# A two-layer encoder trunk in split-fp32 products: transposes of a pair's statistics reordered, last squares added by VectorE, operands and reloads hooked to other multiplies

## The chip, the cores and the metric

The kernel runs on one core of a Trainium2 chip. The metric is the device time of one execution in microseconds (us). A core has TensorE for matrix products (PE in the profile; PEld is its weight load), VectorE (DVE), ScalarE (ACT), GpSimd (POOL) and SyncE (SP), which here issues nearly all DMAs, in one order. Each engine runs its own instructions in order, and semaphores tie the engines together.

## What is computed

Two layers over 2048 tokens of width 1024, in float32, and a last norm:

```python
def reference(x, norm_even, w_in_even, conv_w, w_out_even, norm_odd, w_in_odd,
              q_gain, k_gain, w_out_odd, final_norm):
    for layer in range(DEPTH):                      # DEPTH = 2
        i = layer // 2
        if layer % 2 == 0:                          # short convolution and Fourier mixer
            x = x + short_conv_fourier_mixer(rms_norm(x, norm_even[i]), w_in_even[i], conv_w[i], w_out_even[i])
        else:                                       # grouped-query attention, 8 q heads, 2 kv heads
            x = x + gqa_axial_mixer(rms_norm(x, norm_odd[i]), w_in_odd[i], q_gain[i], k_gain[i], w_out_odd[i])
    return rms_norm(x, final_norm)

def rms_norm(x, g):
    return x * lax.rsqrt(jnp.mean(x * x, axis=-1, keepdims=True) + EPS) * g
```

Each mixer is one input projection, the mixing itself, and one output projection, whose result is added to x. The change concerns the first layer's output projection (with the residual add), the second layer's input projection, and the second layer's output projection. The norm that follows an output projection needs, for every token, the sum of the squares of its 1024 new values.

## The kernel before

**Products.** Tokens lie in four blocks of 512 (tb 0 to 3), and two blocks make a pair (pr 0 or 1). Activations are kept transposed (features on partitions). An operand is a float32 tile split in a high and a low part: ScalarE casts the high part (`split`, L42), VectorE subtracts it for the low part (L44). A product is three matmuls (L58, L59, L60). A projection is worked off in chunks: one pair of token blocks against 512 columns. A plain chunk has 8 block multiplies of 24 matmuls 128x512 each (a11 w11, a12 w21, a21 w11, a22 w21, a11 w12, ...). A fast chunk (`product`) does the same with 7 multiplies in the manner of Strassen and Winograd: the operands are "11", "s2", "s3", "s1", "12", "22", "s4", in this order, where s1 to s4 are sums and differences of the four blocks. Its results are finished in the order: block "22" (after the multiply s1), "11" (after 12), "21" (after 22), "12" (after s4). The first digit of a result block is the token block of the pair, the second the half of the columns.

**Where operands come from.** `load_block` loads a block of the activations (a11 and so on, two halves each) and splits it; `reload` hooks four such loads onto four multiplies of a chunk (a hook runs behind its multiply in program order). `prepare` returns four steps for a pair: s3a, s3b (the halves of s3 and s2, L285 on GpSimd, L288 on VectorE), s1 (L296 on GpSimd: block 22 + block 21, two halves) and s4 (L304 on GpSimd: block 12 minus s2, which is stored in DRAM in between as s2_y0 and so on). In each of them one source block is loaded straight into the operand's own tile and the other into a place of a ring with three places (ring_o). There are nine large tiles: two are the rings (ring_o, and ring_r for raw weights), seven are operands. So in a plain chunk whose four blocks are all live, three of the four combined operands have a tile at once, and the fourth one's loads wait for the last multiply that reads a block that is given up (a21).

**Statistics.** `out_chunk` adds the residual to each result block, and for its two halves ScalarE squares them (L1035, into a tile sq of a pool with two buffers) and GpSimd adds the squares into a sum per token block, acc (L1037). When a pair's two chunks (mc 0 and 1) are done, `rstd(tb)` transposes the sum of a token block on TensorE (four transposes, pm_n, L96), VectorE reduces it, and GpSimd takes the power. In the first layer's output projection there are four chunks: 0 (pr 0, plain), 1 (pr 0, fast), 2 (pr 1, plain), 3 (pr 1, fast); rstd(0) and rstd(1) are hooked onto the first two multiplies of chunk 2. rstd(2) and rstd(3) are hooked onto the second and fourth multiply of the next stage's first chunk (a z chunk). The second layer's output projection has chunks 0 (plain), 1 (fast) and 2 (plain, rstd(0) behind its first and rstd(1) behind its third multiply), and then single columns.

**Order.** TensorE's order is the program's. The orders of the other engines and of the DMAs of SP come from a scheduler, so a hook that stands elsewhere can move other instructions too.

**Names.** po are results of an output projection (po_p, po_u, po_v, po_w are tiles of a fast chunk's running sums, L461; L1016 and L1018 add the residual), wo and w the weights' split tiles, a_y, as_y, a_x, as_x, a_o plain and combined operands of the three projections, pq and pz results of the q and z (gate) columns, ptq the transposes of q, yT, x1T, oT tensors in DRAM.

## Time and profile before

| | |
|---|---|
| median of 3 runs | 2344.59 us (2343.51 to 2349.03) |
| profiled execution | 2344.58 us, its span 2342.8 us |
| PE busy | 2251.1 us, 96% of the span |
| DVE busy | 1694.0 us, 72% |
| ACT busy | 1264.6 us, 54% |
| POOL busy | 720.9 us, 31% |
| mean granted clock of TensorE | 0.982 |

An instruction's row gives its start, its length, its engine and line, what it writes and reads, and in brackets how long its engine was idle just before it and what ended that. The profiled execution and the median differ by 0.01 us. What TensorE's busy time leaves of the span is 91.7 us.

### The profile page before, as it was taken

The numbers are of one execution on the slowest core, as the hardware profiler recorded it, in microseconds if no ns is written. First come the engines' busy times: TensorE is split into PE (matmuls) and PEld (weight loads), VectorE is DVE, ScalarE is ACT, GpSimd is POOL, SyncE is SP. The second block draws the span as 40 slices with busy tenths as digits, with TensorE's granted clock in tenths as the row PEclk, the third lists the DMA queues.
The fourth block names the chain that finished last, engine by engine and source line by source line (L and its number), as shares of the span: only waits on it lengthen the run. The fifth ranks groups of instructions, "written<-read, shape, count | busy, mean of one in ns | idle before, by whom it ended". The sixth has DMA issues, their size and how long they took to land. (4 is left out here: it accounts for less than half of the span.)

```text
span 2342.8 us, 34481 instructions
## 1 busy us (share of the span) xinstructions
PE 2251.1 (96%) x12330; PEld 1905.7 (81%) x12330; DVE 1694.0 (72%) x2557; ACT 1264.6 (54%) x2713; POOL 720.9 (31%) x458
## 2 busy tenths in 40 slices
PE   9999899998989899999999999999999999999988
PEld 7877678877768699899977888888888888888867
DVE  7967667679776546765657888788787787887755
ACT  5442332223343346555537777777777777776422
POOL 3566434343654315424501111000001100013532
PEclk9999999998999999999999999999999999999989
DMA  4245732175897744575476555555555555558873
GB/s 164 84 151 178 240 125 72 63 268 191 293 291 235 221 138 149 195 246 172 152 238 239 202 203 201 192 202 196 198 200 191 200 204 192 204 186 296 283 247 109
DMA packets 268028, 457.53 MB, mean 195 GB/s; under 512 B 26192, under 2 KB 146128, under 8 KB 266064
## 3 DMA queue, kind: packets, MB, share of 16 engines
q1 hardware_dynamic: 260976, 447.63, 56.0%
q0 software_dynamic: 1008, 6.55, 0.7%
q8 instruction: 98, 1.61, 0.3%
q10 hardware_dynamic: 5872, 1.14, 0.2%
q14 instruction: 74, 0.61, 0.1%
HBM read 228.67 MB, written 92.36 MB: 137 GB/s over the span
## 5 line engine op out<-in xcount | busy, mean ns | idle before, releaser
L1410 DVE TENSOR_REDUCE mx<-s 128x1 f32<-128x512 f32 x512 | 350.9, 686 | 173.1 <-PE s L60 172.8
L1429 ACT ACTIVATE praw<-s,nb,qs 128x512 f32<-128x512 f32 x512 | 400.7, 798 | 18.6 <-DVE nb L1419 12.5
L1452 ACT CAST pr<-t 128x512 fp32r<-128x512 f32 x512 | 290.2, 599 | 182.5 <-PE t L1440 182.5
L1456 DVE TENSOR_TENSOR pr<-t,pr 128x512 fp32r<-128x512 f32 x512 | 329.2, 679 | 7.5 <-ACT pr L1452 7.2
L1440 PEld LDWEIGHTS t<-ident_r,P 128*128 128x128 f32 x2048 | 202.0, 140 | 36.8 <-DVE pr L1456 1.1
L58 PE MATMUL s<-kv,aq 128*128 128x512 f32 x512 | 211.0, 412 | 2.8 <-DMA aq<-qT 1.5
L58 PE MATMUL o<-pr,kv 128*128 128x512 f32 x512 | 212.2, 415 | 0.1
L1440 PE MATMUL t<-ident_r,P 128*128 128x128 f32 x2048 | 203.7, 243 | 0.9 <-DVE pr L1456 0.9
L60 PE MATMUL o<-pr,kv 128*128 128x512 f32 x512 | 202.5, 396 | 0.0
L59 PE MATMUL o<-pr,kv 128*128 128x512 f32 x512 | 202.2, 395 | 0.0
L60 PE MATMUL s<-kv,aq 128*128 128x512 f32 x512 | 202.0, 394 | 0.0
L59 PE MATMUL s<-kv,aq 128*128 128x512 f32 x512 | 201.0, 392 | 0.0
L1501 POOL TENSOR_TENSOR az<-az,lb 128x512 f32<-128x512 f32 x32 | 59.1, 1846 | 438.5 <-DMA lb<-ld 438.5
L1508 POOL TENSOR_TENSOR az<-az,oc 128x512 f32<-128x512 f32 x32 | 41.3, 1291 | 288.6 <-ACT oc L1507 288.6
L1037 POOL TENSOR_TENSOR acc<-acc,sq 128x512 f32<-128x512 f32 x48 | 81.5, 1700 | 129.4 <-ACT sq L1035 113.8
L60 PEld LDWEIGHTS o<-pr,kv 128*128 128x128 f32 x512 | 96.3, 188 | 23.2
L60 PEld LDWEIGHTS s<-kv,aq 128*128 128x128 f32 x512 | 96.1, 188 | 22.4
L58 PEld LDWEIGHTS s<-kv,aq 128*128 128x128 f32 x512 | 95.9, 187 | 21.7 <-ACT praw L1429 3.2
L1429 ACT ACTIVATION_READ_ACCUMULATOR praw<-s,nb,qs 128x1 f32 x512 | 112.4, 220 | 0.0
L59 PEld LDWEIGHTS o<-pr,kv 128*128 128x128 f32 x512 | 96.6, 189 | 17.1
L59 PEld LDWEIGHTS s<-kv,aq 128*128 128x128 f32 x512 | 96.4, 188 | 17.1
L58 PEld LDWEIGHTS o<-pr,kv 128*128 128x128 f32 x512 | 96.1, 188 | 16.9 <-ACT oc L1507 0.2
(774 smaller groups left out, 6162.8 us busy)
## 6 DMA issues: line engine op xcount, KB each, us to landing
P<-praw SPq DMA_DIRECT2D x256, 512.0 KB, 3.2
ring_r<-w SPq DMA_DIRECT2D x80, 512.0 KB, 4.0
ring_o<-x_T SPq DMA_DIRECT2D x32, 512.0 KB, 4.8
ring_r<-wo SPq DMA_DIRECT2D x32, 512.0 KB, 7.6
qT<-ring_o SPq DMA_DIRECT2D x64, 256.0 KB, 2.9
aq<-qT SPq DMA_DIRECT2D x31, 512.0 KB, 4.6
a_x<-x1T SPq DMA_DIRECT2D x18, 512.0 KB, 6.1
as_y<-yT SPq DMA_DIRECT2D x16, 512.0 KB, 7.8
```

Of the source, the lines that this page charges most:

```text
L58: nc.tensor.matmul(ps, lh, rh, start=first, stop=False, skip_group_check=shared)
L59: nc.tensor.matmul(ps, lh, rl, start=False, stop=False, skip_group_check=shared)
L60: nc.tensor.matmul(ps, ll, rh, start=False, stop=last, skip_group_check=shared)
L1037: nc.gpsimd.tensor_tensor(a, a, sq, op=ALU.add)
L1410: self.nc.vector.tensor_reduce(st.mx[h][:, b:b + 1], st.banks[h, b][:], op=ALU.max, axis=AX.X)
L1429: self.exp = nc.scalar.activation(raw[:, b % 2], st.banks.pop((h, b))[:], AF.Exp, bias=st.nb[h][:], scale=self.c.qs[:, st.g[0], st.g[1], h ...
L1440: self.nc.tensor.transpose(pt[:, h * P:(h + 1) * P].bitcast(F32R), st.Ps[h // 2][:, h % 2, kt // 8, (kt % 8) * P:(kt % 8 + 1) * P], self.c ...
L1452: self.nc.scalar.copy(pr[:, 0], pt[:])
L1456: self.nc.vector.tensor_tensor(pr[:, 1], pt[:], pr[:, 0], op=ALU.subtract)
L1501: nc.gpsimd.tensor_tensor(zt, zt, rb[:].rearrange("p (t h) -> p h t", h=4), op=ALU.mult)
L1508: nc.gpsimd.tensor_tensor(st.zt[:], st.zt[:], o[:], op=ALU.mult)
```

## The change

Four things are changed.

- In a fast chunk the squares of the blocks "21" and "12" are added by VectorE, the others still by GpSimd (12 of 48 adds move).
- The transposes of a pair's sums change places: rstd(1) behind the first and rstd(0) behind the second multiply in chunk 2 of the first output projection, and the same in chunk 2 of the second one (the finishing of these blocks, `finish`, is exchanged with them). In the z chunk rstd(3) is behind the fourth and rstd(2) behind the sixth multiply.
- The steps of `prepare` are hooked elsewhere. First output projection: s3a, s3b, s4, s1 behind multiplies 2, 4, 6, 7 of the plain chunk (counted from 0; s3a, s3b, s1, s4 behind 0, 2, 4, 6 before). Second input projection: s3a, s3b, s1 behind 0, 2, 4 of the first q chunk (1, 3, 6 before), and s4 behind the multiply "11" of the fast z chunk (behind 6 of the second q chunk before).
- `reload` hooks its four blocks onto "s3", "12", "22", "s4" of a fast chunk (onto "11", "s2", "s3", "s1" before), and the load of block 2 for the last stage (x2_2, 2 MB) hooks onto "s1" (onto "22" before).

```diff
         def s4():
-            self.A.pop("21")
+            self.A.pop("21", None)
...
         if last:
-            A = dict(self.A)
+            A = {a: self.A[a] for a in A_OPS if a in self.A}
             self.A.clear()
         for a in ("11", "s2", "s3", "s1", "12", "22", "s4"):
             base = ps.get({"12": "11", "s4": "s1"}.get(a))
-            ps[a] = self.multiply(A.pop(a) if last else A[a], W[W_OPS[a]], f"{name}{a}", base, a in ("11", "s1"))
+            ps[a] = self.multiply((A if a in A else self.A).pop(a) if last else A[a], W[W_OPS[a]], f"{name}{a}", base, a in ("11", "s1"))
...
             if not first:
-                nc.gpsimd.tensor_tensor(a, a, sq, op=ALU.add)
+                eng = nc.vector if kind == "fast" and block in ("21", "12") else nc.gpsimd
+                eng.tensor_tensor(a, a, sq, op=ALU.add)
...
-            hooks = {0: s3a, 2: s3b, 4: s1, 6: s4}
+            hooks = {2: s3a, 4: s3b, 6: s4, 7: s1}
             if pr:
-                hooks.update({0: lambda: (rstd(0), s3a()), 1: lambda: rstd(1)})
+                hooks.update({0: lambda: rstd(1), 1: lambda: rstd(0)})
         else:
             src, name = ([c.yT[2], c.yT[3]], "y1") if pr == 0 else ([c.x1T[0], c.x1T[1]], "x0")
-            hooks = st.reload(src, name, ("11", "s2", "s3", "s1"))
+            hooks = st.reload(src, name, ("s3", "12", "22", "s4"))
...
-            q_chunk(pr, n, W, {1: s3a, 3: s3b, 6: s1})
+            q_chunk(pr, n, W, {0: s3a, 2: s3b, 4: s1})
         elif n == 1:
-            q_chunk(pr, n, W, {6: s4})
+            q_chunk(pr, n, W, {})
         elif i == 0:
-            z_chunk(pr, n - 2, W, {1: lambda: c.rstd1(2), 3: lambda: c.rstd1(3)})
+            z_chunk(pr, n - 2, W, {3: lambda: c.rstd1(3), 5: lambda: c.rstd1(2)})
         else:
             src = [c.x1T[2], c.x1T[3]]
-            hooks = st.reload(src, "x1", ("11", "s2", "s3", "s1")) if i == 4 else {"s3": lambda: st.load_block(src, "21", "x1")}
-            z_chunk(pr, n - 2, W, hooks, "fast")
+            hooks = st.reload(src, "x1", ("s3", "12", "22", "s4")) if i == 4 else {"12": lambda: st.load_block(src, "21", "x1")}
+            z_chunk(pr, n - 2, W, {"11": s4, **hooks}, "fast")
...
-            x = st.pair("ro"[1 - tb])
+            x = st.pair("ro"[tb])
...
         if i == 1:
-            hooks = {**st.reload([c.oT[2], c.oT[3]], "o1", ("11", "s2", "s3", "s1")), "22": lambda: load_x(2)}
+            hooks = {**st.reload([c.oT[2], c.oT[3]], "o1", ("s3", "12", "22", "s4")), "s1": lambda: load_x(2)}
         if i == 2:
-            hooks = {0: lambda: (load_x(3), rstd(0)), 2: lambda: rstd(1), 4: lambda: finish(0)}
+            hooks = {0: lambda: (load_x(3), rstd(1)), 1: lambda: rstd(0), 4: lambda: finish(1)}
...
         if m == 1:
-            finish(1)
+            finish(0)
```

**Place 1.** VectorE at the end of the fast chunk 1 of the first output projection (po0_0_1 are its results, wo0_2 the next chunk's weights, acc0_0 the pair's sums), before:

```order
L1018 TENSOR_TENSOR po0_0_1_v_4674<-po0_0_1_v_4674,ring_o_4269 128x1024
L44 TENSOR_TENSOR wo0_2_12l_4791<-ring_r_3974,wo0_2_12h_4790 128x1024
L461 TENSOR_TENSOR po0_0_1_u_4630<-po0_0_1_u_4630,po0_0_1_s1_0_4677 128x512
L461 TENSOR_TENSOR po0_0_1_u_4630<-po0_0_1_u_4630,po0_0_1_s1_1_4678 128x512
L1018 TENSOR_TENSOR po0_0_1_u_4630<-po0_0_1_u_4630,ring_o_4269 128x1024
L44 TENSOR_TENSOR wo0_2_22l_4830<-ring_r_3974,wo0_2_22h_4829 128x1024
```

The same place of the change:

```order
L1018 TENSOR_TENSOR po0_0_1_v_4660<-po0_0_1_v_4660,ring_o_4273 128x1024
L44 TENSOR_TENSOR wo0_2_12l_4784<-ring_r_3974,wo0_2_12h_4783 128x1024
L1038 TENSOR_TENSOR acc0_0_4329<-acc0_0_4329,sq0_1_4_4792 128x512
L1038 TENSOR_TENSOR acc0_0_4329<-acc0_0_4329,sq0_1_5_4795 128x512
L461 TENSOR_TENSOR po0_0_1_u_4616<-po0_0_1_u_4616,po0_0_1_s1_0_4663 128x512
L461 TENSOR_TENSOR po0_0_1_u_4616<-po0_0_1_u_4616,po0_0_1_s1_1_4664 128x512
L1018 TENSOR_TENSOR po0_0_1_u_4616<-po0_0_1_u_4616,ring_o_4273 128x1024
L44 TENSOR_TENSOR wo0_2_22l_4830<-ring_r_3974,wo0_2_22h_4829 128x1024
L1038 TENSOR_TENSOR acc0_0_4329<-acc0_0_4329,sq0_0_6_4838 128x512
L1038 TENSOR_TENSOR acc0_0_4329<-acc0_0_4329,sq0_0_7_4841 128x512
```

The four adds stand behind one weight split each, and nothing else moved here. The sums of token block 1 (sq0_1) are complete before those of token block 0.

**Place 2.** SP at the end of the plain chunk 0 of the first output projection, where the operands of the first fast chunk are loaded (y0; s2_y0 is the stored s2). Before:

```order
L218 DMA ring_o_4269<-yT_60 128x2x512
L303 DMA ring_o_4269<-s2_y0_4242 128x1024
L1028 DMA x1T_61<-po0_0_0_t_4460 128x2x512
L1026 DMA ring_o_4269<-x_T 128x2x512
L218 DMA as4_y0_4498<-yT_60 128x2x512 x2
L303 DMA ring_o_4269<-s2_y0_4242 128x1024
L315 DMA ring_r_3974<-wo0 128x4x256
```

The same stretch of the change, with the rows that follow:

```order
L290 DMA s2_y0_4242<-ring_o_4273 128x1024
L218 DMA ring_o_4273<-yT_60 128x2x512
L218 DMA as1_y0_4538<-yT_60 128x2x512 x2
L303 DMA ring_o_4273<-s2_y0_4242 128x1024
L315 DMA ring_r_3974<-wo0 128x4x256
L1028 DMA x1T_61<-po0_0_0_t_4526 128x2x512
L1026 DMA ring_o_4273<-x_T 128x2x512
L315 DMA ring_r_3974<-wo0 128x4x256
L1026 DMA ring_o_4273<-x_T 128x2x512
L218 DMA a11_y1_4645<-yT_60 128x2x512 x2
L218 DMA ring_o_4273<-yT_60 128x2x512
```

The operand whose loads wait for a21's tile was s4 and is now s1, and the second half of block 22 for s1 (the last row) goes to ring_o behind the stored s2 and the first loads of the next chunk.

**Place 3.** VectorE at the end of the fast chunk 1 of the second output projection (po1_0_1 its results, a22_o1 the next chunk's operand block, acc1_0 the pair's sums), before:

```order
L44 TENSOR_TENSOR a22_o1_20942<-a22_o1_20942 128x1024
L1016 TENSOR_TENSOR po1_0_1_p_20828<-ring_o_20508,po1_0_1_11_0_20791 128x512
L1016 TENSOR_TENSOR po1_0_1_p_20828<-ring_o_20508,po1_0_1_11_1_20792 128x512
L44 TENSOR_TENSOR a22_o1_20942<-a22_o1_20942 128x1024
L44 TENSOR_TENSOR wo1_2_21l_20990<-ring_r_20278,wo1_2_21h_20989 128x1024
L461 TENSOR_TENSOR po1_0_1_v_20913<-po1_0_1_v_20913,po1_0_1_22_0_21003 128x512
L461 TENSOR_TENSOR po1_0_1_v_20913<-po1_0_1_v_20913,po1_0_1_22_1_21004 128x512
L1018 TENSOR_TENSOR po1_0_1_v_20913<-po1_0_1_v_20913,ring_o_20508 128x1024
L44 TENSOR_TENSOR wo1_2_12l_21033<-ring_r_20278,wo1_2_12h_21032 128x1024
```

The same place of the change:

```order
L461 TENSOR_TENSOR po1_0_1_v_20899<-po1_0_1_v_20899,po1_0_1_22_0_20992 128x512
L461 TENSOR_TENSOR po1_0_1_v_20899<-po1_0_1_v_20899,po1_0_1_22_1_20993 128x512
L44 TENSOR_TENSOR wo1_2_12l_21026<-ring_r_20278,wo1_2_12h_21025 128x1024
L1018 TENSOR_TENSOR po1_0_1_v_20899<-po1_0_1_v_20899,ring_o_20508 128x1024
L44 TENSOR_TENSOR a22_o1_21064<-a22_o1_21064 128x1024
L1038 TENSOR_TENSOR acc1_0_20554<-acc1_0_20554,sq1_1_4_21034 128x512
L461 TENSOR_TENSOR po1_0_1_u_20855<-po1_0_1_u_20855,po1_0_1_s1_0_20902 128x512
L461 TENSOR_TENSOR po1_0_1_u_20855<-po1_0_1_u_20855,po1_0_1_s1_1_20903 128x512
L1038 TENSOR_TENSOR acc1_0_20554<-acc1_0_20554,sq1_1_5_21037 128x512
L44 TENSOR_TENSOR a22_o1_21064<-a22_o1_21064 128x1024
```

The split of the last block a22_o1 came ahead of the weight part wo1_2_21l before; now its first half stands between the residual add of po1_0_1_v and the first of the adds on VectorE, and its second half behind the second add.

## Rows read from the trace of the kernel before

**Rows 1.** The page's busy times over the whole span.

```profile
PE 2251.1 (96%) x12330; PEld 1905.7 (81%) x12330; DVE 1694.0 (72%) x2557; ACT 1264.6 (54%) x2713; POOL 720.9 (31%) x458
```

**Rows 2.** Waits of TensorE over the whole span: line, what it waited for: us in total, times, the longest.

```profile
PE pm_n L96 <- POOL acc L1037: 26.8, 3, 11.4
PE ptq L1137 <- POOL pq_t L1127: 6.2, 3, 3.1
```

**Rows 3.** Timeline of TensorE, at eight places in order of time: start, length, line, what it writes and reads, and the idle time ahead with what ended it. The rows at 651.56 and 794.13 are the first matmuls of a block multiply.

```profile
604.07 0.79 PE L59 MATMUL po<-a_y,wo_21h 128*128 128x512 f32 x1 [4.09 <-DVE a_y L44]
...
651.56 0.39 PE L58 MATMUL po_s<-as_y,wo_t1h 128*128 128x512 f32 x1
...
687.63 1.11 PE L96 MATMUL pm_n<-ident,acc 128*128 128x128 f32 x4 [8.45 <-POOL acc L1037]
...
786.81 1.11 PE L96 MATMUL pm_n<-ident,acc 128*128 128x128 f32 x4 [6.94 <-POOL acc L1037]
...
794.13 0.39 PE L58 MATMUL pz<-a_x,w_21h 128*128 128x512 f32 x1
...
799.63 0.60 PE L96 MATMUL pm_n<-ident,acc 128*128 128x128 f32 x4
...
987.15 0.50 PE L58 MATMUL pz_s<-as_x,w_t1h 128*128 128x512 f32 x1 [2.63 <-DVE pz_u L461]
...
2241.26 1.11 PE L96 MATMUL pm_n<-ident,acc 128*128 128x128 f32 x4 [11.45 <-POOL acc L1037]
```

**Rows 4.** Stretches of the span at the lower granted clock, one row each: from and to, length, busy time of PE, PEld, DVE, ACT, POOL with the number of instructions, granted clock as a share of the full one, DMA share, GB/s.

```profile
601.90:608.70 6.80, 4.63 (x10) 3.31 (x11) 6.80 (x6) 1.99 (x2) 1.56 (x1) 0.50 0.32 109
683.80:690.60 6.80, 2.96 (x9) 2.57 (x10) 5.08 (x5) 2.09 (x2) 4.54 (x4) 0.50 1.06 385
782.80:789.60 6.80, 2.79 (x9) 2.41 (x10) 3.79 (x7) 2.21 (x3) 5.28 (x5) 0.50 1.06 392
987.60:991.00 3.40, 3.40 (x10) 2.62 (x9) 3.40 (x5) 3.19 (x5) 0.00 (x0) 0.50 0.45 155
1124.20:1127.60 3.40, 3.40 (x18) 3.40 (x17) 0.72 (x2) 3.27 (x16) 2.38 (x1) 0.50 0.90 308
2233.50:2247.20 13.70, 5.94 (x16) 4.88 (x17) 6.07 (x7) 2.76 (x5) 6.46 (x5) 0.50 1.06 390
```

**Rows 5.** Timeline of GpSimd at the end of the fast chunk 1 of the first output projection and the start of chunk 2. Like instructions that follow each other are one row (x6).

```profile
668.21 12.63 POOL L1037 TENSOR_TENSOR acc<-acc,sq 128x512 f32<-128x512 f32 x6 [16.18 <-ACT sq L1035]
680.81 3.32 POOL L285 TENSOR_TENSOR ring_o<-as_y,ring_o 128x1024 f32<-128x1024 f32 x1
684.09 3.49 POOL L1037 TENSOR_TENSOR acc<-acc,sq 128x512 f32<-128x512 f32 x2
```

**Rows 6.** Timeline of VectorE in the same stretch.

```profile
674.95 2.32 DVE L44 TENSOR_TENSOR wo_12l<-ring_r,wo_12h 128x1024 fp32r<-128x1024 f32 x1
677.19 1.27 DVE L461 TENSOR_TENSOR po_u<-po_u,po_s 128x512 f32<-128x512 f32 x2
678.50 1.22 DVE L1018 TENSOR_TENSOR po_u<-po_u,ring_o 128x1024 f32<-128x1024 f32 x1
679.64 2.29 DVE L44 TENSOR_TENSOR wo_22l<-ring_r,wo_22h 128x1024 fp32r<-128x1024 f32 x1
```

**Rows 7.** The adds of squares: on GpSimd over the whole span (count, then shortest, median and longest in ns), and VectorE's add of the same shape in the last stage (busy us, mean ns).

```profile
L1037 POOL TENSOR_TENSOR acc<-acc,sq x48: 1260/1482/2332, 612.8 to 2293.6; 128x512 f32<-128x512 f32 x48
...
L1635 DVE TENSOR_TENSOR acc<-acc,sq 128x512 f32<-128x512 f32 x4 | 2.8, 691 | 2.2 <-ACT sq L1633 2.2
```

**Rows 8.** The second output projection: the last two adds on GpSimd, a residual add on VectorE, and the issue of the two halves of the last operand block (a22) on SP.

```profile
2238.41 2.79 POOL L1037 TENSOR_TENSOR acc<-acc,sq 128x512 f32<-128x512 f32 x2 [1.88 <-ACT sq L1035]
...
2230.59 2.33 DVE L1018 TENSOR_TENSOR po_v<-po_v,ring_o 128x1024 f32<-128x1024 f32 x1
...
2215.72 0.97 SPq L218 DMA_DIRECT2D a_o<-oT  x2
```

**Rows 9.** The operand s4 of the first fast chunk (y0), from the issue of its loads to its last split: SP, GpSimd (the second half), VectorE; then all loads of two kinds (count, KB each, median us from issue to landing).

```profile
631.08 2.07 SPq L218 DMA_DIRECT2D as_y<-yT  x2
...
641.56 2.42 POOL L304 TENSOR_TENSOR ring_o<-as_y,ring_o 128x1024 f32<-128x1024 f32 x1 [0.22 <-DMA ring_o<-s_y]
...
642.46 4.86 DVE L44 TENSOR_TENSOR as_y<-ring_o,as_y 128x1024 fp32r<-128x1024 f32 x2 [3.63 <-ACT as_y L42]
...
as_y<-yT SPq DMA_DIRECT2D x16, 512.0 KB, 7.8
...
ring_o<-yT SPq DMA_DIRECT2D x12, 512.0 KB, 8.4
```

**Rows 10.** GpSimd and VectorE ahead of TensorE's wait at 604.07.

```profile
597.32 2.87 POOL L285 TENSOR_TENSOR ring_o<-as_y,ring_o 128x1024 f32<-128x1024 f32 x1
...
597.84 3.43 DVE L44 TENSOR_TENSOR as_y<-ring_o,as_y 128x1024 fp32r<-128x1024 f32 x1
601.19 2.82 DVE L44 TENSOR_TENSOR a_y<-ring_r,a_y 128x512 fp32r<-128x512 f32 x1
```

**Rows 11.** GpSimd and VectorE ahead of TensorE's wait at 987.15, in the fast z chunk.

```profile
976.25 2.50 POOL L304 TENSOR_TENSOR ring_o<-as_x,ring_o 128x1024 f32<-128x1024 f32 x1
...
981.99 1.22 DVE L44 TENSOR_TENSOR as_x<-ring_o,as_x 128x1024 fp32r<-128x1024 f32 x1
986.42 0.67 DVE L461 TENSOR_TENSOR pz_u<-pz_p,pz_s 128x512 f32<-128x512 f32 x1
```

## The prediction

> **What bounds the kernel now.** I read the busy times first: TensorE is at work for 96% of the span and no other engine for more than 72% [rows 1]. So only the time in which TensorE stands, and the time in which it runs slowly, can be won. Then the waits of TensorE: the transposes of the statistics (pm_n) waited three times, 26.8 us in all, for GpSimd's add of a square, the largest item by far; the transposes of q waited 6.2 us [rows 2]. The timeline gives the places: 8.45 us ending at 687.63, 6.94 at 786.81 and 11.45 at 2241.26, and beside them 4.09 at 604.07 and 2.63 at 987.15 [rows 3]. Last the granted clock: around each of these waits lies a stretch at 0.50, that is at the lower of the two levels (1.2 instead of 2.4 GHz) [rows 4]. In it a matmul takes twice its time, so half of TensorE's busy time in such a stretch is lost on top of the wait. With that the five places cost: 604: 4.1 + 4.63/2 = 6.4. 687: 8.45 + 2.96/2 = 9.9. 786: 6.94 + 2.79/2 = 8.3. 987: 2.63 + 3.40/2 = 4.3. 2241: 11.45 + 5.94/2 = 14.4. A full-speed block multiply takes 799.63 - 794.13 = 5.5 us [rows 3].
>
> **The three waits for the sums.** At 687 the first transposes were asked for at 687.63 - 8.45 = 679.2. GpSimd had then still to do two adds, one L285 and two adds [rows 5]; six adds took 12.63 us, 2.1 each. In the change GpSimd has four of them, done at 668.2 + 4 x 2.1 = 676.6, and the sums of token block 1, which are complete first, are now transposed first. VectorE does its two adds behind wo_12l, which ended at 677.3 [rows 6]. An add of that shape takes it 0.69 us [rows 7], so they end at 678.7, before 679.2: no wait. The other two stand behind two sums (1.27), the residual add (1.22) and wo_22l (2.29) [rows 6], plus 1.4: 684.9. The second transposes are due one multiply and one set of transposes later, 679.2 + 5.5 + 0.4 = 685.1. No wait again, but with 0.2 us to spare. The bounds: nothing if all goes so; if each add costs VectorE what it cost GpSimd at worst, 2.33 [rows 7], the first pair ends at 682.0 (2.8 late) and the second 3 us late as well. I take the low end, as VectorE's own row is the nearer one: **-9.9**. The adds delay what stands behind them on VectorE, the weight part and the next operands, by 1.4 us per pair; 3.3 us and more of slack lie there, since wo_22l is first read by the fourth multiply, 11 us after the second transposes.
>
> A rule of the Trainium skill speaks against this (SBUF — State Buffer, section Who interferes with whom): a VectorE instruction with two SBUF inputs and a GpSimd instruction that reads SBUF exclude each other for a whole instruction. By it an add that meets L285 stands for up to its 3.32 us, and this term would be some 3 us smaller. The trace agrees in kind: beside GpSimd's adds the split wo_12l took 2.32 us, while a residual add of the same size took 1.22 [rows 6].
>
> At 786 the transposes of block 2 leave the second multiply for the sixth, 22 us later, and those of block 3 stay behind the fourth, 11 us after; the sums were ready 6.94 us late. Both are covered: **-8.3**. What is then late is the reduction, the power and the tables that wait for the sum's tile, and they are wanted by the k columns only after the eighth multiply.
>
> At 2241 the transposes were asked for at 2229.8, and GpSimd's last adds began at 2238.41 [rows 8]. Now the first adds on VectorE stand behind the first half of a22's split. Its loads were issued at 2215.72 [rows 8]; in the change the 2 MB of x2_2 go ahead of them, 5.4 us at the 390 GB/s of that stretch [rows 4], so about 2221. A load of that size lands between half of 7.8 us, the median of as_y [rows 9], and all of it, then come a cast (1.1), a split (1.2 to 2.3), an add, two sums and an add (2.7): ready between 2229.9 and 2234.9, that is 0 to 5 us late. I take 2.5 and 0.5 for the clock; the second transposes have a multiply more: **-11.4** of 14.4.
>
> **The wait at 604.** The second L285 (2.87 us from 597.32) ran beside two VectorE instructions that took 3.43 and 2.82 us [rows 10]; a split of the first one's size takes about 1.2 when nothing runs beside it (the residual add, 1.22 [rows 6]). L285 is hooked later, so both should shrink, by up to 4 us; but the weight differences (L342) follow on GpSimd in its place. I take 2 us of the wait and 0.5 of the clock: **-2.5**, between 0 and 6.4.
>
> **The q and z chunks.** At risk or to be won are 4.3 (987) plus 6.2 for the q transposes plus 3.40/2 for the stretch at 1124: 12.2 us [rows 2 to 4]. At 987 TensorE waited for pz_u at 986.42, behind a split of s4 at 981.99 and one of a_x; GpSimd's L304 of s4 stood ahead of the transposes' operand [rows 11]. All of s4 now comes after the multiply "11", so most of that goes. In the q chunks the halves of s3, s2 and s1 leave VectorE's queue earlier, but s1's two GpSimd steps (2.4 us each, as L304) now stand next to the q products. I take 4.3 + 2.2: **-6.5**, between +3 and -12.
>
> **The new wait.** In the first fast chunk the operand that waits for a21's tile was s4, read last; it is now s1, read fourth, from 651.56 [rows 3]. s4's second half was split at 642.46 + 4.86 = 647.3 [rows 9], in time for s4 at 668. In the change the second half of block 22 for s1 can be loaded only when the stored half for s4 has left its ring place, which is at that split, so about 648. Then a load (8.4 us is the median of the kind [rows 9], I take 5, as only two loads stand ahead of it), GpSimd's sum 2.42 [rows 9], cast 1.1, split 1.2: about 657.7. TensorE wants that half in the middle of the multiply, 651.56 + 2.75 = 654.3. Late by 3.4 (0, if the ring place is free earlier, to 6.8 with 8.4); with a clock loss like those at 604 and 987 (2): **+5.5**, between 0 and 9. In the second fast chunk both loads of s1 stand early, and I count nothing.
>
> **Sum.** -9.9 - 8.3 - 11.4 - 2.5 - 6.5 + 5.5 = -33.1 from 2344.6 (the profiled execution, 0.01 off the median): **2311.5 us**. All moves of finish, ring places and x2_2 lie off TensorE's path; they cost nothing as long as x2_2 is read 2 multiplies later than it lands.
>
> **Rivals.**
> - *The adds stay late on VectorE.* If they cost the upper bounds above, 687 keeps 2.8 + 3 and a clock loss of 1.5, and 2241 another 5: 12 us more, 2324. For it: the 0.2 us to spare at 685, and the stretched splits in rows 6. Against: GpSimd has nothing but L285 there after 676.6. The rule of the Trainium skill weighed above (SBUF — State Buffer, Who interferes with whom) would bring it about.
> - *No new wait.* If s1's second half comes in time, and 604 and 2241 vanish entirely: 2311.5 - 5.5 - 3.9 - 3.0 = 2299. For it: s4's second half took only 16 us from issue to split [rows 9], which would serve s1 by 648. Against: the ring's third user.
> - *Slower: VectorE blocked at the head of its queue.* Its adds wait for squares whose two buffers are freed by GpSimd's adds. If VectorE stands for w ahead of each pair of adds, all splits behind them shift by 2w in each of three chunks; from w = 33/6 = 5.5 us the gain is gone, at 8 us it is 2311.5 + 48 = 2359. For it: two buffers, and a split per add pair behind it. Against: GpSimd is done at 676.6, before VectorE arrives at 677.3.
> - *Nothing measurable.* The waits at TensorE were for something else than the adds, or gains and new waits cancel: about 2344. Against it stands that GpSimd's last add ended, at 684.09 + 3.49 = 687.58, just ahead of the transposes [rows 5].
>
> **Numbers.** Chances: forecast 0.58 (2303 to 2320), late adds 0.18, no new wait 0.12, blocked VectorE 0.08, nothing 0.04. The range takes the forecast's unknowns and reaches to 2299 and 2328. No change, to what this kernel's runs can tell, is within 0.3%, 7 us: faster 0.88, same 0.05, slower 0.07.
>
> **What would show it.** Right: no row of pm_n <- acc over 1 us at chunk 2 of the first projection nor in the z chunk; one of 1 to 5 us in the second projection; a wait of po_s on as_y of 2 to 6 us near 650; 987 gone. Wrong: pm_n waiting for a VectorE acc by several us, several new waits for as_y, a_y or a_o, or more stretches at 0.50 than before.

## The result, and the profile of the changed kernel

The changed kernel took 2326.72 us (median of 4, 2323.19 to 2327.72) against 2345.51 us (4 runs) for the kernel before: a ratio of 0.9916 (95% interval 0.9898 to 0.9933), 18.8 us faster. The forecast was 2311.5 with a range of 2299 to 2328: the direction and the range hold, the latter by 1.3 us, the size is some 0.57 of what was forecast, and the time lies outside the 2303 to 2320 to which the forecast gave a chance of 0.58. The profiled spans are 2325.8 and 2342.8 us, 17.0 apart; they are compared below.

The page's busy times after, to be read beside [rows 1]:

```profile
PE 2249.2 (97%) x12330; PEld 1903.7 (82%) x12330; DVE 1705.1 (73%) x2569; ACT 1264.4 (54%) x2713; POOL 702.2 (30%) x446
```

TensorE's work is the same (2251.1 before); the time comes from its waits. These are the waits after, in the form of [rows 2] (total, times, longest):

```profile
PE po_s L59 <- DVE as_y L44: 6.9, 2, 5.1
PE pm_n L96 <- DVE acc L1038: 6.2, 1, 6.2
PE po L59 <- DVE a_y L44: 4.7, 2, 4.0
PE ptq L1138 <- POOL pq_t L1128: 3.6, 2, 1.8
PE po_s L58 <- ACT as_y L42: 1.7, 2, 1.2
PE po_s L60 <- DVE wo_t3l L44: 1.6, 1, 1.6
```

Of 26.8 us for the sums 6.2 are left, in one place. New are the rows of po_s: the s operands of the first projection, 10.2 us with the weight part wo_t3l. The timeline of TensorE after shows where, in the order of time; the rows of pm_n without brackets are transposes that waited for nothing, in the places of [rows 3] at 687 and 786:

```profile
605.01 0.50 PE L59 MATMUL po<-a_y,wo_21h 128*128 128x512 f32 x1 [3.97 <-DVE a_y L44]
...
657.49 0.50 PE L58 MATMUL po_s<-as_y,wo_t1h 128*128 128x512 f32 x1 [0.58 <-ACT as_y L42]
663.10 0.79 PE L59 MATMUL po_s<-as_y,wo_t1h 128*128 128x512 f32 x1 [5.11 <-DVE as_y L44]
...
689.74 0.60 PE L96 MATMUL pm_n<-ident,acc 128*128 128x128 f32 x4
...
695.68 0.60 PE L96 MATMUL pm_n<-ident,acc 128*128 128x128 f32 x4
...
742.30 0.51 PE L60 MATMUL po_s<-as_y,wo_t3l 128*128 128x512 f32 x1 [1.60 <-DVE wo_t3l L44]
748.78 0.49 PE L58 MATMUL po_s<-as_y,wo_t1h 128*128 128x512 f32 x1 [1.16 <-ACT as_y L42]
751.10 0.51 PE L59 MATMUL po_s<-as_y,wo_t1h 128*128 128x512 f32 x1 [1.83 <-DVE as_y L44]
...
808.90 0.60 PE L96 MATMUL pm_n<-ident,acc 128*128 128x128 f32 x4
...
2225.42 1.11 PE L96 MATMUL pm_n<-ident,acc 128*128 128x128 f32 x4 [6.23 <-DVE acc L1038]
```

Two stretches of the change at a granted clock of 0.50, beside the waits at s1 and in the second projection, columns as in [rows 4] (the one at 604 is there as before, those at 683, 782, 987 and 1124 are gone):

```profile
660.70:667.50 6.80, 4.40 (x10) 3.47 (x11) 5.20 (x6) 1.44 (x2) 0.00 (x0) 0.50 0.49 155
2224.00:2230.80 6.80, 5.38 (x15) 4.41 (x16) 6.64 (x10) 2.10 (x4) 1.14 (x1) 0.50 1.06 386
```

**Where the 17.0 us came from.** The start of the same block multiply in both traces gives an offset, after minus before; its steps are the worth of each place, the slow clock included:

| place (time before) | forecast | traces |
|---|---|---|
| ahead of the first changed hook | 0 | +1.1 |
| 604, chunk 0 | -2.5 | +1.4 |
| s1 of the first fast chunk (654) | +5.5 | +8.3 |
| 687, transposes in chunk 2 | -9.9 | -10.2 |
| second fast chunk (740 to 771) | 0 | +6.2 |
| 786, z chunk | -8.3 | -8.6 |
| q and z chunks (987 and the q transposes) | -6.5 | -8.5 |
| 2241, second output projection | -11.4 | -5.4 |
| attention and the end | 0 | -1.2 |
| sum | -33.1 | -16.9 |

So two terms came as forecast (687 and 786), a third was larger (q and z), and the missing 16 us lie in four places: 6.2 in the second fast chunk, 6.0 in the second output projection, 3.9 at 604 and 2.8 at s1 (18.9), less 2.0 of more gain in the q and z chunks and 0.7 in the rest. These are steps between two single traces; at 500 us, ahead of the first changed hook, the twelve traces of this study lie some 3 us apart at most although every engine's order is the same up to there, so a step of 1 to 2 us shows little.

### The profile page after: what moved, and what is told of

It is laid out like the page before. It is cut to its first block, busy times and chain, and to the rows that moved or that the text cites. A ratio compares the mean times of both kernels' runs of the same rounds, so it can differ in the third digit from the quotient of the medians.

```text
span 2325.8 us, 34488 instructions
## 1 busy us (share of the span) xinstructions
PE 2249.2 (97%) x12330; PEld 1903.7 (82%) x12330; DVE 1705.1 (73%) x2569; ACT 1264.4 (54%) x2713; POOL 702.2 (30%) x446
## 5 line engine op out<-in xcount | busy, mean ns | idle before, releaser
L58 PEld LDWEIGHTS o<-pr,kv 128*128 128x128 f32 x512 | 96.0, 187 | 16.9 <-ACT oc L1508 0.2
L1038 POOL TENSOR_TENSOR acc<-acc,sq 128x512 f32<-128x512 f32 x36 | 65.8, 1831 | 96.9 <-ACT sq L1035 96.0
```

What stands on the lines that cost most here:

```text
L58: nc.tensor.matmul(ps, lh, rh, start=first, stop=False, skip_group_check=shared)
L1038: eng.tensor_tensor(a, a, sq, op=ALU.add)
```

## The experiments

The theory after the comparison was: the order of the transposes does what was forecast; the s operands of the first projection became late by their new places, and cost 14.5 us; and in the second projection VectorE's own queue, not its two adds, holds the sums back. The rivals: the adds on VectorE are what counts; it is the order of s4 ahead of s1, not its lateness, that costs; in the second projection the transfers are late. Each ratio below is to runs of the kernel before in the same batch.

**The operands of the first projection.** First s1 ahead of s4 at the change's late places:

```diff
-            hooks = {2: s3a, 4: s3b, 6: s4, 7: s1}
+            hooks = {2: s3a, 4: s3b, 6: s1, 7: s4}
```

> The changed kernel (2326.7 us) with one edit: in the first output projection s1 is hooked ahead of s4 again (s3a, s3b, s1, s4 behind multiplies 2, 4, 6, 7). Theory A, that s1 is late because it now is the operand that waits for a21's tile and for the ring place of s4's stored half: the waits of TensorE for as_y in the multiply s1 of chunks 1 and 3 (8.3 and 5.4 us with their slow clock in the changed kernel) go, s4 comes in time, and the time is 2311 to 2316 us. Theory B, that all combined operands are late because s3a and s3b are hooked two multiplies later: waits of the same size stay at s1 or move to s4, 2322 to 2329 us.

It took 2327.53 us, ratio 0.9923 (0.9900 to 0.9946). No wait at s1 is left in either fast chunk, but two others came up, at chunk 2's transposes and in the second fast chunk's s4:

```profile
686.00 0.68 PE L96 MATMUL pm_n<-ident,acc 128*128 128x128 f32 x4 [2.64 <-DVE acc L1038]
...
763.10 0.47 PE L58 MATMUL po_s<-as_y,wo_22h 128*128 128x512 f32 x1 [2.96 <-ACT w_11h L327]
```

The gain at s1 was real in the trace and did not last: TensorE came to these two places 6.4 and 7.5 us earlier than in the change, and met the next producers before they were done. Next s4 ahead of s1 as in the change, but both at the places of the kernel before (0, 2, 4, 6):

```diff
-            hooks = {2: s3a, 4: s3b, 6: s4, 7: s1}
+            hooks = {0: s3a, 2: s3b, 4: s4, 6: s1}
             if pr:
-                hooks.update({0: lambda: rstd(1), 1: lambda: rstd(0)})
+                hooks.update({0: lambda: (rstd(1), s3a()), 1: lambda: rstd(0)})
```

> The changed kernel with one edit: s3a, s3b, s4, s1 behind multiplies 0, 2, 4, 6, that is the hooks of the kernel before with s4 ahead of s1. Theory A (the order of s1 and s4): the waits at s1 stay at 8 us or more in the two fast chunks together, 2321 to 2330 us. Theory B (the later hooks): they go, 2311 to 2316 us. The wait at 605 stays at 4 to 6 us by both.

2317.94 us, ratio 0.9893 (0.9874 to 0.9913): below the change by 9 us in the medians and 5 in the ratios, whose intervals still overlap (the change: 0.9898 to 0.9933), and above the 2311 to 2316 that was expected of it. There is no wait at s1 or s3 in either fast chunk. The order by itself is not the cause of these waits, then. Here are, from SP and VectorE of this kernel, the second split of s4 and the load for s1 that takes its ring place:

```profile
635.18 1.23 DVE L44 TENSOR_TENSOR as_y<-ring_o,as_y 128x1024 fp32r<-128x1024 f32 x1 [4.04 <-ACT as_y L42]
...
636.44 0.36 SPq L218 DMA_DIRECT2D ring_o<-yT  x1
```

In the change the same two stand at 647.14 and 649.37. The dependence that the forecast followed is there in both; 13 us earlier it is harmless. Either remedy, the old order or the old time, removes the wait.

**The adds and the order of the transposes.** The change with all adds back on GpSimd:

```diff
-                eng = nc.vector if kind == "fast" and block in ("21", "12") else nc.gpsimd
+                eng = nc.gpsimd
```

> The changed kernel with all adds of squares on GpSimd again, the order of the transposes as changed. If the adds on VectorE are what removed the waits for the sums, two of them come back in part: 2 to 6 us at chunk 2 of the first projection, 6 to 12 us instead of 6.2 at the second projection, 2330 to 2340 us. If the order of the transposes (and the delay by the wait at s1, which gives GpSimd time) is enough, no wait for the sums at chunk 2 of the first projection, 6 to 8 us at the second, 2326 to 2331 us.

2328.01 us, ratio 0.9937 (0.9920 to 0.9953). No wait of pm_n in chunk 2 or the z chunk, and 7.65 us instead of 6.23 in the second projection. But the waits at s1 ahead of chunk 2 gave GpSimd some 8 us, so this run cannot tell about chunk 2. The change with the old order of the transposes in both output projections (and `finish` with it):

```diff
-                hooks.update({0: lambda: rstd(1), 1: lambda: rstd(0)})
+                hooks.update({0: lambda: rstd(0), 1: lambda: rstd(1)})
...
-            x = st.pair("ro"[tb])
+            x = st.pair("ro"[1 - tb])
...
-            hooks = {0: lambda: (load_x(3), rstd(1)), 1: lambda: rstd(0), 4: lambda: finish(1)}
+            hooks = {0: lambda: (load_x(3), rstd(0)), 2: lambda: rstd(1), 4: lambda: finish(0)}
...
-            finish(0)
+            finish(1)
```

> The changed kernel with the old order of the transposes in the two output projections (block 0 first), the adds on VectorE as changed, the z chunk as changed. The adds of block 0 ended 0.2 us before the first transposes were due in the first projection and 10 to 11 us after it in the second. If the adds alone are enough in the first projection, no wait of more than 1.5 us there; in the second the wait grows from 6.2 to 10 or 11 us, its slow stretch by 1 to 2: 2330 to 2334 us. If the order is what counts in both, 4 to 6 us more in the first too: 2335 to 2340 us.

2333.33 us, ratio 0.9957 (0.9942 to 0.9972), with a wait of 12.9 us in the second projection and none in chunk 2, where the waits at s1 had again given time. Both edits were therefore made again on the kernel without the s1 waits (the second one above). The adds on GpSimd there:

> Kernel e2_s4_first_early with all adds of squares on GpSimd. Here no wait at s1 gives GpSimd time. If the adds on VectorE are needed at chunk 2 of the first projection, waits for the sums of 2 to 7 us come back there (both transposes together, with the slow clock), and 1 to 3 us more at the second projection: 2321 to 2328 us. If the order of the transposes is enough, no wait over 1 us there: 2318 to 2321 us.

2316.21 us, ratio 0.9875 (0.9850 to 0.9899): not slower. The three waits of its transposes:

```profile
683.05 0.66 PE L96 MATMUL pm_n<-ident,acc 128*128 128x128 f32 x4 [0.48 <-POOL acc L1038]
...
689.89 0.66 PE L96 MATMUL pm_n<-ident,acc 128*128 128x128 f32 x4 [0.66 <-POOL acc L1038]
...
2220.33 1.12 PE L96 MATMUL pm_n<-ident,acc 128*128 128x128 f32 x4 [7.82 <-POOL acc L1038]
```

The adds on VectorE save 1.1 us of waiting in chunk 2 and 1.4 us at the last place (6.47 there with the adds on VectorE), and the time as a whole doesn't show it. TensorE came to chunk 2 some 3.4 us later here than in the kernel before, GpSimd to its adds there only 1.7 (669.88 against 668.21), which shortens these waits. The old order of the transposes on the same kernel:

> Kernel e2_s4_first_early with the old order of the transposes in the two output projections, the adds on VectorE. The sums of block 0 end 4 to 5 us after the first transposes are due in the first projection: a wait of 4 to 5 us and 1.5 for the clock there, and 12 to 13 instead of 6.5 at the second one with 2 us of clock: 2327 to 2333 us. If the adds alone are enough in the first projection, no wait there: 2322 to 2327 us.

2330.99 us, ratio 0.9938 (0.9918 to 0.9959), 10 us more by the ratios and 13 by the medians; the waits are back although VectorE does its adds:

```profile
686.29 1.11 PE L96 MATMUL pm_n<-ident,acc 128*128 128x128 f32 x4 [5.96 <-DVE acc L1038]
...
2225.21 1.12 PE L96 MATMUL pm_n<-ident,acc 128*128 128x128 f32 x4 [11.77 <-DVE acc L1038]
```

Last the order alone, on the kernel before: adds on GpSimd, every operand and reload at its old place.

```diff
-                hooks.update({0: lambda: (rstd(0), s3a()), 1: lambda: rstd(1)})
+                hooks.update({0: lambda: (rstd(1), s3a()), 1: lambda: rstd(0)})
...
-            z_chunk(pr, n - 2, W, {1: lambda: c.rstd1(2), 3: lambda: c.rstd1(3)})
+            z_chunk(pr, n - 2, W, {3: lambda: c.rstd1(3), 5: lambda: c.rstd1(2)})
...
-            x = st.pair("ro"[1 - tb])
+            x = st.pair("ro"[tb])
...
-            hooks = {0: lambda: (load_x(3), rstd(0)), 2: lambda: rstd(1), 4: lambda: finish(0)}
+            hooks = {0: lambda: (load_x(3), rstd(1)), 1: lambda: rstd(0), 4: lambda: finish(1)}
...
-            finish(1)
+            finish(0)
```

> The kernel before with one thing of the change alone: the statistics of a pair are transposed block 1 (or 3) first in all three places (both output projections and the z chunk of layer 1), with the places of the transposes, the reduction and its ring place that go with it; all adds stay on GpSimd, and all hooks of operands and reloads stay where they were. Theory O (the order is what earns; the places of the operands earn or lose little): the 8.45 us wait in chunk 2 of the first output projection falls to under 1.5 us, the 6.94 us one in the z chunk goes, the 11.45 us one in the second output projection falls to 5 to 8 us, the waits at 604 and 987 and the three of the q transposes stay, no wait comes at s1; in all -9 -8.3 -5 = 20 to 24 us off, 2321 to 2326 us. Theory P (the order only works with the adds on VectorE or with the operands placed later, since GpSimd still has the L285 of the next chunk ahead of its last adds): the wait in chunk 2 stays at 4 us or more and the second projection at 9 or more; 2330 to 2335 us.

2325.09 us, ratio 0.9916 (0.9893 to 0.9939): as much as the whole change. Its transposes in both output projections (those of the z chunk wait for nothing), between them a wait in the second fast chunk, and GpSimd in chunk 2:

```profile
681.32 0.66 PE L96 MATMUL pm_n<-ident,acc 128*128 128x128 f32 x4
688.15 0.66 PE L96 MATMUL pm_n<-ident,acc 128*128 128x128 f32 x4 [0.67 <-POOL acc L1037]
...
758.25 0.57 PE L58 MATMUL po_s<-as_y,wo_22h 128*128 128x512 f32 x1 [3.50 <-DVE po_w L461]
...
2223.65 1.11 PE L96 MATMUL pm_n<-ident,acc 128*128 128x128 f32 x4 [5.64 <-POOL acc L1037]
```

```profile
668.33 12.93 POOL L1037 TENSOR_TENSOR acc<-acc,sq 128x512 f32<-128x512 f32 x6 [16.02 <-ACT sq L1035]
681.22 3.40 POOL L285 TENSOR_TENSOR ring_o<-as_y,ring_o 128x1024 f32<-128x1024 f32 x1
684.58 3.52 POOL L1037 TENSOR_TENSOR acc<-acc,sq 128x512 f32<-128x512 f32 x2
```

GpSimd's stretch is that of [rows 5] within half a microsecond. Its six adds end just as the first transposes are due; L285 and the last two adds lie behind one whole multiply of TensorE, and 8.45 us of wait become 0.67. Some of that is owed to TensorE, which was 2.1 us later in this trace (lost at 604), while GpSimd was not: at 679.2, when the transposes were asked for in the kernel before, the six adds still had until 680.84 to go [rows 5]. The wait of 3.50 us at 758.25, for po_w in the last multiply of the second fast chunk, makes most of the 3.9 us that this chunk lost by the offset of the traces. Four kernels whose engines have the same order up to there (e2_s4_first_early, f1_x2_late, f2_o1_early, g1_q_old) lose 0.4, 2.9, 2.4 and 2.3 us in it; what sets it was not tested.

**The second output projection.** On the kernel without the s1 waits, the 2 MB of x2_2 behind the third of the four operand blocks' loads (hook "22" instead of "s1"; those of the last block still follow it):

```diff
-            hooks = {**st.reload([c.oT[2], c.oT[3]], "o1", ("s3", "12", "22", "s4")), "s1": lambda: load_x(2)}
+            hooks = {**st.reload([c.oT[2], c.oT[3]], "o1", ("s3", "12", "22", "s4"))}
+            hooks["22"] = lambda f=hooks["22"]: (f(), load_x(2))
```

> Kernel e2_s4_first_early (2317.9 us, no wait at s1) with one edit: the 2 MB load of x2_2 is hooked behind the multiply 22 again. Theory C, that in the second projection the sums are late because these 2 MB go ahead of the last three operand blocks, so that VectorE waits for a12 and has the splits left when the adds come: the wait of the transposes there falls from 6.5 to 0 to 3 us, 2311 to 2315 us. Theory D, that VectorE's queue has the splits of a21 and a22 and a weight part ahead of the adds whenever they land: the wait stays at 5 to 8 us, 2316 to 2320 us.

2318.28 us, ratio 0.9885 (0.9863 to 0.9906); the wait is 5.07 instead of 6.47 us. And the reloads of this chunk at the places of the kernel before, x2_2 too, which now comes behind all of them:

```diff
-            hooks = {**st.reload([c.oT[2], c.oT[3]], "o1", ("s3", "12", "22", "s4")), "s1": lambda: load_x(2)}
+            hooks = {**st.reload([c.oT[2], c.oT[3]], "o1", ("11", "s2", "s3", "s1")), "22": lambda: load_x(2)}
```

> Kernel e2_s4_first_early with the reloads of the second projection's operand blocks hooked behind 11, s2, s3, s1 again, and x2_2 behind 22. Theory D (splits ahead of the adds): no split stands between the residual add and the adds any more, the wait falls from 6.5 to 0 to 3 us, 2311 to 2315 us. Theory E, that VectorE is busy without a gap there in any order: the residual adds come as late as in the kernel before, and the wait is 4 to 7 us, 2315 to 2320 us.

2318.79 us, ratio 0.9886 (0.9864 to 0.9908), wait 4.78 us. So a later x2_2 is worth 1.4 us of the wait, 1.7 together with the old places of the reloads, and neither shows in the time. VectorE in the changed kernel, from the last but two operand halves to the second add:

```profile
2208.17 1.23 DVE L44 TENSOR_TENSOR a_o<-a_o 128x1024 fp32r<-128x1024 f32 x1 [2.16 <-ACT a_o L42]
...
2213.81 4.56 DVE L44 TENSOR_TENSOR a_o<-a_o 128x1024 fp32r<-128x1024 f32 x2
...
2220.62 1.21 DVE L1018 TENSOR_TENSOR po_v<-po_v,ring_o 128x1024 f32<-128x1024 f32 x1
2221.76 1.21 DVE L44 TENSOR_TENSOR a_o<-a_o 128x1024 fp32r<-128x1024 f32 x1
2222.89 0.68 DVE L1038 TENSOR_TENSOR acc<-acc,sq 128x512 f32<-128x512 f32 x1
...
2224.69 0.68 DVE L1038 TENSOR_TENSOR acc<-acc,sq 128x512 f32<-128x512 f32 x1
```

The transposes were asked for at 2225.42 - 6.23 = 2219.19. The residual add of the block that they need ran at 2220.62, behind splits of operands and weights; from 2208.17 on VectorE has hardly a gap. In the kernel with the order alone, where the adds follow on GpSimd, the wait is 5.64. Whoever adds last, the block itself comes late out of VectorE's queue. This is read off the trace, with the transfers ruled out; no run took work off VectorE at this place.

**The q and z chunks.** On the kernel without the s1 waits, the s operands of the second input projection at their old places:

```diff
-            q_chunk(pr, n, W, {0: s3a, 2: s3b, 4: s1})
+            q_chunk(pr, n, W, {1: s3a, 3: s3b, 6: s1})
...
-            q_chunk(pr, n, W, {})
+            q_chunk(pr, n, W, {6: s4})
...
-            z_chunk(pr, n - 2, W, {"11": s4, **hooks}, "fast")
+            z_chunk(pr, n - 2, W, hooks, "fast")
```

> The kernel with s4 ahead of s1 and both two multiplies earlier (2318 us), and the combined operands of the q and z chunks of layer 1 back at the places of the kernel before (s3 behind the multiplies 1 and 3, s1 behind 6 of the first q chunk, s4 behind 6 of the second). Theory Q (those places earn what the two traces' difference showed, 8.5 us, by the wait before the z chunk's first s operand and the q transposes): the wait of about 2.6 us for pz_u near 985 is back with its stretch at 0.50, the waits of the q transposes for GpSimd are 6 us instead of 3.6; 2324 to 2328 us. Theory R (the gain there came from the other parts, since the s1 operand and the wait move with the start of the stage): under 3 us more, 2317 to 2321 us, no wait over 1.5 us near 985.

2321.83 us, ratio 0.9917 (0.9895 to 0.9940). The wait that the change removed is back:

```profile
974.27 0.51 PE L58 MATMUL pz_s<-as_x,w_t1h 128*128 128x512 f32 x1 [2.38 <-DVE pz_u L461]
```

The stretch at 0.50 that was expected behind it did not come, and the q transposes wait 4.4 us in all where 6 were expected and 3.7 are left in the kernel without this edit. The medians are 3.9 us apart, the ratios 0.0024, or 5.6 us, with intervals that overlap (the kernel without this edit ends at 0.9913); the offsets of the two traces give 6.7 in these chunks. So the wait and its cause are shown, the size is not: 4 to 7 us, which the times alone would not tell from nothing, and below the 8.5 read off one pair of traces.

## Why the prediction was right in sign and too large

- **687 and 786 (-9.9, -8.3): right**, with -10.2 and -8.6. The step that fell is the reason given for 687: the four adds taken from GpSimd were counted as needed, and the order alone does nearly all of it (0.67 us of wait left, in a trace in which TensorE came 2.1 us later). The working had GpSimd's two blocks of work in [rows 5] and the due times of both transposes; it did not try the new order with the old adds. Its 0.2 us to spare were not tested in the change: the wait at s1 ahead gave VectorE time, and the adds ended at 684.58 and 689.56, the transposes began at 689.74 and 695.68. In e2_s4_first_early, without that wait, the second pair ended at 688.17 and its transposes began at 688.23: as tight as forecast. VectorE's adds took 0.68 to 0.69 us, as assumed from [rows 7].
- **The rule of the Trainium skill** weighed there (SBUF — State Buffer, section Who interferes with whom) was not put to the test in chunk 2: GpSimd's L285 began at 691.27 and met none of the adds, as the timeline of GpSimd and VectorE after shows:

```profile
673.33 8.76 POOL L1038 TENSOR_TENSOR acc<-acc,sq 128x512 f32<-128x512 f32 x4 [17.10 <-ACT sq L1035]
691.27 2.41 POOL L285 TENSOR_TENSOR ring_o<-as_y,ring_o 128x1024 f32<-128x1024 f32 x1 [9.18 <-DMA ring_o<-yT]
...
683.10 1.48 DVE L1038 TENSOR_TENSOR acc<-acc,sq 128x512 f32<-128x512 f32 x2
...
688.08 1.48 DVE L1038 TENSOR_TENSOR acc<-acc,sq 128x512 f32<-128x512 f32 x2
```

  The comparison that the prediction gave for the rule misread its rows: the residual add of 1.22 us, at 678.50, ran beside GpSimd's adds as well as the split of 2.32 us did (668.21 to 680.84 [rows 5]), so it is no measure of a VectorE instruction alone, here or in the term for 604. It agrees with the rule in another way: the GpSimd add that began 0.01 us behind it took 2.33 us, the longest of the 48 in [rows 7]. Where VectorE did stand beside GpSimd's adds, in the second projection, the trace agrees in kind: two splits took 4.56 us from 2213.81 on (shown above), against 1.21 for one at 2221.76, when GpSimd, at its four adds until 2217.28, was done:

```profile
2208.81 8.47 POOL L1038 TENSOR_TENSOR acc<-acc,sq 128x512 f32<-128x512 f32 x4 [13.33 <-ACT sq L1035]
```

- **s1 of the first fast chunk (+5.5): the right wait, undersized at +8.3.** The chain came as worked out: ring place free at 649.34, load issued at 649.37, GpSimd and ScalarE done at 657.43. The step that failed is the last, "split 1.2: about 657.7". VectorE's queue held it for 4.4 us more, which the chain had left out. TensorE itself wanted the operand 2.6 us later than forecast (656.91 for 654.3), having lost that time ahead of it, or the wait would have been longer. The timeline of VectorE after, with that split as the last row:

```profile
653.87 4.58 DVE L44 TENSOR_TENSOR a_y<-a_y 128x1024 fp32r<-128x1024 f32 x2
658.37 1.27 DVE L461 TENSOR_TENSOR po_v<-po_u,po_s 128x512 f32<-128x512 f32 x2
659.57 1.21 DVE L44 TENSOR_TENSOR wo_22l<-ring_r,wo_22h 128x1024 fp32r<-128x1024 f32 x1
660.70 1.21 DVE L44 TENSOR_TENSOR a_y<-a_y 128x1024 fp32r<-128x1024 f32 x1
661.84 1.21 DVE L44 TENSOR_TENSOR as_y<-ring_o,as_y 128x1024 fp32r<-128x1024 f32 x1
```

- **The second fast chunk ("I count nothing"): wrong, +6.2.** The premise that both loads of s1 stand early is what failed. On SP they come behind a load that waits for s4's second half, and that one waited for s2 to go to DRAM and back. From the timeline of SP (s2's store and reload), GpSimd, VectorE and SP again (the two loads), after:

```profile
722.31 0.38 SPq L290 DMA_DIRECT2D s_y<-ring_o  x1
730.39 0.32 SPq L303 DMA_DIRECT2D ring_o<-s_y  x1
...
735.27 2.40 POOL L304 TENSOR_TENSOR ring_o<-as_y,ring_o 128x1024 f32<-128x1024 f32 x1 [3.67 <-DMA ring_o<-s_y]
...
738.79 1.23 DVE L44 TENSOR_TENSOR as_y<-ring_o,as_y 128x1024 fp32r<-128x1024 f32 x1 [3.66 <-ACT as_y L42]
...
740.04 0.36 SPq L218 DMA_DIRECT2D ring_o<-yT  x1
740.50 0.94 SPq L218 DMA_DIRECT2D as_y<-yT  x2
```

  That split also stood ahead of wo_t3l on VectorE, which is the 1.60 at 742. With the hooks two multiplies earlier none of these waits for s operands is there.
- **The second output projection (-11.4): half, -5.4.** Forecast were 2.5 us late between 0 and 5, and 0.5 for the clock; measured 6.23 and 5.38/2 = 2.7. The wait passed even the upper bound. The working followed one chain, the last operand block's loads, and with x2_2 behind these the wait was only 1.7 us shorter; the residual add behind VectorE's other work was not in it. The clock term was taken too low without a row for it: the stretches of [rows 4] at such waits cost 1.4 to 3.0.
- **604 (-2.5): not shown, +1.4.** The step moved was not the cause, or not alone: the wait here, the slow clock left out, is 2.0 to 4.8 us in the four kernels with L285 moved and 2.9 to 5.9 in the eight with it in place, the kernel before among them. This place scatters by more than the term: it is 3.7, 5.5, 5.0 and 5.9 us in the four kernels named above whose engines have the same order up to there. What sets it stays open.
- **q and z (-6.5): right in place**, 987 gone and the q transposes down from 6.2 to 3.6; between -4 and -8.5 by the traces and medians, not clear of noise by the ratios.

Of the rivals, "late adds" gave the nearest time (2324) for a reason that did not occur; "VectorE blocked" did not occur: no add on VectorE in the change had more than 0.11 us of idle time ahead of it. Of the signs named beforehand for a wrong forecast two came, pm_n waiting several us for an add on VectorE (6.23) and several new waits for as_y; the stretches at 0.50 became fewer, not more. The statement that decided the study is that the order of the transposes alone gives the change's 0.9916: the better q and z chunks (4 to 8.5 us) and the adds (2.5 us of waiting) were paid away again in the two fast chunks of the first projection, which lost 14.5 us by the traces against 3.9 with the order alone. With the s operands at their old times the kernel runs at 0.9893, and at 0.9875 with the adds on GpSimd. Both lie below the change, but their intervals still touch or overlap its own, and the two are not told apart.

## What to carry to other kernels

When a consumer waits for several sums that are completed one after the other, ask for them in the order of their completion before making the producer faster: here a whole multiply of cover came for nothing, and a quicker engine for the last adds gained 2.5 us of waiting in the traces and nothing that the times show. A chain of dependences gives only the earliest time; each step on a busy engine also stands behind what is queued there, and on VectorE at 73% that was 4.4 us in a chain of 14. Moving a producer later to thin out one stretch has to be followed through every later use of its buffers, in each repetition of the loop, since the second may start with less slack than the first.

## What the runs showed of the hardware

- The same add of 128x512 took VectorE 0.68 to 0.69 us nearly everywhere (median 692 ns of 12; the longest, 1821, ran beside an instruction of GpSimd, L1101, in the z chunk) and GpSimd 1.3 to 2.4 (median 1890 of 36), as the rows of this line over the whole span of the change show (count, then shortest, median and longest in ns):

```profile
L1038 POOL TENSOR_TENSOR acc<-acc,sq x36: 1287/1890/2365, 614.2 to 2274.1; 128x512 f32<-128x512 f32 x36
...
L1038 DVE TENSOR_TENSOR acc<-acc,sq x12: 676/692/1821, 683.1 to 2230.4; 128x512 f32<-128x512 f32 x12
```

- The longer waits were paid for twice: 5.7 us of waiting at s1 came to 8.3 with the slow clock behind it, and 6.23 in the second projection to 8.9, an estimate that adds half of TensorE's 5.38 us of busy time in the stretch at 0.50. Three waits of 1.60, 1.16 and 1.83 us in the second fast chunk had no such stretch behind them; two of 1.21 and 0.71 us in the same chunk of g1_q_old had one (3.4 us from 758.1).
